# A two-layer encoder kernel: guest splits pinned to three points of each up-projection step, their stores on GpSimd's queue, and modulation dots moved beside the input projection

## The chip, the cores and the metric

The kernel runs on one core of a Trainium2 chip. The metric is the device time of one execution in microseconds. Three runs were timed and their median is used. A hardware profile of one further execution gives the busy times, waits and single instructions below. Engines are named as in the profile: PE is TensorE, PEld its weight loads, DVE is VectorE, ACT is ScalarE, POOL is GpSimd, SP is SyncE, which here only issues DMAs.

## The reference

The reference is an encoder of two layers over 1024 positions of 1024 channels. Each layer takes a modulation vector of six parts from a conditioning vector `c`, mixes along the sequence (attention in layer 0, a long-convolution mixer in layer 1), and then runs a gated feed-forward network whose gate passes a convolution of three taps.

```python
for i in range(DEPTH):
    mod = (silu(c) @ ada_w[i] + ada_b[i])[:, None, :]
    sh1, sc1, g1, sh2, sc2, g2 = jnp.split(mod, 6, axis=-1)
    h = rmsnorm(x, norm1_g[i]) * (1.0 + sc1) + sh1
    y = attention_mixer(h, ...) if i == 0 else hyena_mixer(h, ...)   # hyena starts with h @ w_in
    x = x + g1 * y
    h = rmsnorm(x, norm2_g[i]) * (1.0 + sc2) + sh2
    gate, val = jnp.split(h @ w_up, 2, axis=-1)
    x = x + g2 * ((silu(dwconv3(gate)) * val) @ w_down)
return rmsnorm(x, final_g)
```

## The kernel before

Everything is float32. A matrix product is made of three products of split operands: each operand is a high part (a cast on ScalarE, for weights `nc.scalar.copy`) and a low part (the difference, a `tensor_tensor` on VectorE, the helper `sub_lo`, L162), and the product of the two low parts is left out. The splits are therefore work for ScalarE and VectorE beside every product of TensorE.

The stages, in order of time: the input norm and the query, key and value projection (channels of weights in the order 2, 0, 1, each over eight tiles `j` of 128 positions); attention; the output projection `wo` over eight row tiles `dt_`; the feed-forward network of layer 0, which is `ffn(0, ...)`; the long-convolution mixer; `ffn(1, ...)`; the final norm.

*The up projection in `ffn`.* It goes over 22 tiles `f` of the hidden width. Two are made plainly. For the other 20 a step of seven products, `product(...)` at L946, gives gate and value with one product fewer (a scheme with sums and differences of the operands). A step loads its weights `u` through SP's queue, casts them in `fill` (L1033, `w_hi`) and subtracts (L162, `w_lo`), adds partial results (`pu`, `cv`), makes the convolution and the Silu of the gate (L287 to L289, L1002), and sends the product to memory (`sg`). The last product of a step and its gating, `late`, run inside the next step.

*Guests.* At three places of a step, `extra(...)` advances a generator once; the work in it is called a guest here. In layer 0 the generator is `l1_work`. It prepares weights of layer 1: 64 half tiles of `w_in` and `w_out` are loaded (`lo_load`, L1204, three buffers `wi_raw`), cast (L1218, `wi_hi`), subtracted (L1219) and their low parts stored to memory (L1220, `wld` and `wold`). 54 advances share the 64 splits, so some take two. In layer 1 the generator is `l1_mod5`, eight modulation dots.

*The order on each engine* comes from the framework's scheduler. It takes the instructions in the order in which the code issues them as their priority, follows a simulated timeline, and may put an instruction earlier on its engine than it stands in the code, where its inputs are there and its engine is free in that simulation. Each engine then runs its instructions in that fixed order. `tc.issue_after(ins)` adds a rule for the instructions issued within the block: those on the engine of `ins` come after `ins`. It does not bound them from above, and says nothing on other engines or on DMA queues.

*Modulation dots.* The 48 parts of layer 1's modulation (six vectors of eight columns) are each one `scalar_tensor_tensor` with a sum on VectorE (`mod_dot`, L197) of 512 KB of `ada_t` against the row silu(c). Where they run: 0 to 15 beside the output projection, two to a turn (`wide_dots`, in halves, L386); 16 to 39 beside the first down projection, after every second row tile; 40 to 47 as guests of the second up projection. In the third channel of the first projection GpSimd makes another modulation vector with `mod_step` (L185 to L190), which adds up in the tile `ssq`; the row of the dots is also held in `ssq`. The weights of a channel and the raw data of `mod_step` come through the same two buffers, `w_raw`.

*The down projection.* Row tiles `dt_` run over groups of hidden tiles; TensorE's sums `d_ps` are added to `xd` on VectorE (L1138). Beside the groups after the first the long filter of layer 1 is made (`filter_gen`: products `f_ps`, then L429 to L437 on VectorE, results to `ed`), one part after every second row tile. The weights of the last group (`wdt`) use the room of the filter's pool, so they are written once the filter is finished.

Of the kernel before, what the change touches and what calls it, by code (L numbers as in the profile page):

```python
# [53 lines left out]
L1_WO, L1_DN = 16, 40  # L54
# [61 lines left out]
def tile_kernel(ctx: ExitStack, tc: tile.TileContext, t: dict):  # L116
# [251 lines left out]
    def wide_dots(S, n):  # L368
        row, bufs = S[0:2], [S[2:4], S[4:6], S[6:8]]
        part = const.tile([P, n], F32, name="m_part")  # L370
# [7 lines left out]
        load(0)  # L378
        load(1)
        for j in range(n):  # L380
            if j + 2 < n:
                load(j + 2)
            i, k = divmod(j, KT)
            for hf, acc in enumerate((mod[:, 1, i, k:k + 1], part[:, j:j + 1])):
                w = bufs[j % 3][hf]
                V.scalar_tensor_tensor(w, w, 1.0, row[hf], op0=MUL, op1=MUL, accum_out=acc)  # L386
            if k == KT - 1:
                V.tensor_tensor(mod[:, 1, i], mod[:, 1, i], part[:, j - k:j + 1], op=ADD)
                mod_bias(1, i)
            yield  # L390
# [217 lines left out]
    with tc.tile_pool(name="qkv", bufs=1) as qp:  # L608
# [56 lines left out]
        todo = []  # L665

# [4 lines left out]
        for ch in (2, 0, 1):  # L671
            w = qkv_w if ch == 2 else [load_split(t["w_qkv"][ch, k2], wq, 4) for k2 in range(4)]
            if ch == 1:
                for k in range(KT):
                    mod_step(2, ssq, k)
            pqs = dict(enumerate(pq0)) if ch == 2 else {}
            for j in range(NT):
                if j not in pqs:
                    pqs[j] = mt("qkv_mm", {2: "AAAABBAA", 0: "AABBAAAA", 1: "AAAABBBB"}[ch][j])
                    tj = slice(j * P, (j + 1) * P)  # L680
                    for k in range(KT):
                        wh, wl = w[k // 2]
# [291 lines left out]
    def ffn(l, base, work, tail, more=None):  # L974
# [15 lines left out]
        fl = []  # L990
# [8 lines left out]
        def gated(f, cv):  # L999
            g = fp.tile([P, L], F32, name="gate", tag="gate")  # L1000
            dwconv(cv, [col(C_FW + (3 * l + i) * NF + f) for i in range(3)], col(C_FB + l * NF + f), g)
            nc.scalar.activation(g, g, AF.Silu)  # L1002
# [35 lines left out]
        for f in range(NPL[l], NF):  # L1038
# [10 lines left out]
            nc.scalar.copy(pu[:, 0], y1_[:, 0:512])  # L1049
# [38 lines left out]
        extra(48)  # L1088
# [34 lines left out]
        for j in range(len(ends) - 1):  # L1123
# [3 lines left out]
            for dt_ in range(KT):  # L1127
# [11 lines left out]
                if l == 0 and dt_ % 2:  # L1139
# [38 lines left out]
    def mod_load(i, pool=None):  # L1178
        raw = raw_tile() if pool is None else pool.tile([P, 1024], F32, name="m_raw", tag="m_raw", bufs=2)
        nc.sync.dma_start(raw, t["ada_t"][2 + i // KT, i % KT])  # L1180
        return raw

    def mod_dots(lo, hi, pool=None):
        w = mod_load(lo, pool)
        for i in range(lo, hi):
            w, wn = mod_load(i + 1, pool) if i < hi - 1 else None, w
            mod_dot(1, i // KT, i % KT, wn, ssq)
            if i % KT == KT - 1:
                mod_bias(1, i // KT)
            yield  # L1190

    def l1_mod5(pool, after):
        V.tensor_copy(ssq[0:1, 0:1], after[0:1, 0:1].bitcast(F32))
        silu_row(ssq)
        yield from mod_dots(L1_DN, 48)

    def l1_work(pool, after):
# [12 lines left out]
        for i in range(L1_STEPS):  # L1210
            while n < (i + 1) * len(los) // L1_STEPS:
# [8 lines left out]
                nc.sync.dma_start(dst[:, cs], raw)  # L1220
# [645 lines left out]
```

## Time and profile before

| | us |
|---|---|
| median of 3 runs | 2997.17 (2996.94 to 3002.17) |
| profiled execution, its own time | 3006.47 |
| span of the profile | 3004.7 |
| busy: TensorE | 2837.0 (94%) |
| busy: VectorE | 2333.3 (78%) |
| busy: ScalarE | 1231.0 (41%) |
| busy: GpSimd | 289.1 (10%) |

The span runs from the first to the last instruction of the profiled execution. A row of a timeline gives start and duration in microseconds, engine, line, operation, and in brackets how long the engine stood idle before it and what it waited for. A row of the waits gives total, number and longest. A row by stretch gives busy time and number of instructions of each engine in it, the granted clock of TensorE and the DMA engines' busy share. Starts are counted from the start of the span.

### The profile page before, as it was taken

Reading aid. Unit: us, or ns where it says so; the run is one execution under the profiler, and the core shown is the slowest. Engines: PE = TensorE matmul, PEld = TensorE weight load, DVE = VectorE, ACT = ScalarE, POOL = GpSimd, SP = SyncE. Lnnn points to the kernel's source line nnn. Section 1 sums busy time; section 2 is a strip of 40 time slices with the busy share of each in tenths; the row PEclk is TensorE's granted clock in tenths of the full one; section 3 lists DMA queues with packets and bytes.
Section 4 is the critical chain, followed back from the end, with each engine's and each line's share of the span. In section 5 each row is a group of like instructions: output and inputs, shape, how many; then the busy total and the mean of one; then the engine's idle time right before and its main releaser. Section 6 shows DMA issues by size and latency. Waiting matters only on the chain.

```text
span 3004.7 us, 36415 instructions
## 1 busy us (share of the span) xinstructions
PE 2837.0 (94%) x13152; PEld 2308.3 (77%) x13152; DVE 2333.3 (78%) x3212; ACT 1231.0 (41%) x2001; POOL 289.1 (10%) x292
## 2 busy tenths in 40 slices
PE   5989999999899999999889999999988999999998
PEld 4867877777777787888777877877867788887887
DVE  7788998867788777888677886788977977777544
ACT  3557888834444333343332233323333433333211
POOL 0064465300000000111000000000000000000000
PEclk9999999999999999999999999999999999999999
DMA  6252232162667323876446664556655422223321
GB/s 229 80 161 52 50 81 57 37 227 104 207 215 233 109 78 112 253 218 189 149 162 208 204 217 165 190 193 194 211 186 208 140 84 84 85 77 131 129 84 57
DMA packets 224777, 439.49 MB, mean 146 GB/s; under 512 B 22131, under 2 KB 117139, under 8 KB 220117
## 3 DMA queue, kind: packets, MB, share of 16 engines
q1 hardware_dynamic: 192788, 407.80, 40.1%
q0 software_dynamic: 31808, 29.37, 4.2%
q8 instruction: 104, 1.70, 0.2%
q14 instruction: 77, 0.62, 0.1%
HBM read 308.09 MB, written 128.99 MB: 145 GB/s over the span
## 4 chain that ended last, share of the span: by engine, by line
PE 55%; DVE 8%; DMA 8%; issue 2%; ACT 1%; SPq 0%; DVEq 0%; ACTq 0%; POOLq 0%
PE w_ps L946 20%; PE d_ps L181 16%; PE u_ps L1306 6%; PE ab_ps L1442 2%; DMA wld<-wi_raw 2%; PE f_ps L486 1%; PE f_ps L181 1%; PE f_ps L487 1%; PE z_ps L1420 1%; PE z_ps L1421 1%; DMA wi_raw<-in_w_in_dram 1%; DMA rd<-fw 1%; PE wout_y L181 1%; PE g_ps L283 1%; PE wout_y L1593 1%
## 5 line engine op out<-in xcount | busy, mean ns | idle before, releaser
L1033 ACT CAST w_hi<-u 128x1024 fp32r<-128x1024 f32 x120 | 125.5, 1047 | 203.8 <-PE w_ps L946 194.0
L162 DVE TENSOR_TENSOR pT_lo<-pt_ps,pT_hi 128x512 fp32r<-128x512 f32 x256 | 167.5, 680 | 46.8 <-ACT pT_hi L761 44.7
L946 PE MATMUL w_ps<-t_h,w_hi 128*128 128x512 f32 x480 | 193.2, 403 | 4.3 <-ACT w_hi L1033 4.0
L181 PE MATMUL d_ps<-s_hi,wd_lo 128*128 128x512 f32 x608 | 194.1, 390 | 0.0
L162 DVE TENSOR_TENSOR w_lo<-u,w_hi 128x1024 fp32r<-128x1024 f32 x120 | 146.6, 1222 | 60.2 <-ACT w_hi L1033 60.1
L181 PE MATMUL d_ps<-s_lo,wd_hi 128*128 128x512 f32 x608 | 193.3, 390 | 0.0
L181 PE MATMUL d_ps<-s_hi,wd_hi 128*128 128x512 f32 x608 | 193.0, 390 | 0.0
L946 PE MATMUL w_ps<-t_l,w_hi 128*128 128x512 f32 x480 | 192.1, 400 | 0.0
L946 PE MATMUL w_ps<-t_h,w_lo 128*128 128x512 f32 x480 | 191.2, 399 | 0.0
L1138 DVE SCALAR_TENSOR_TENSOR xd<-d_ps,mod,xd 128x1024 f32<-128x1024 f32 x104 | 132.6, 1279 | 71.8 <-PE d_ps L181 71.4
L761 ACT CAST pT_hi<-pt_ps 128x512 fp32r<-128x512 f32 x256 | 145.1, 589 | 70.7 <-PE pt_ps L756 63.4
L740 DVE TENSOR_REDUCE nmx<-s_ps 128x1 f32<-128x1024 f32 x128 | 155.4, 1215 | 11.1 <-PE s_ps L733 9.2
L756 PE MATMUL pt_ps<-ident,p_t 128*128 128x128 f32 x1024 | 154.6, 275 | 9.3 <-DVE pT_lo L162 9.0
L756 PEld LDWEIGHTS pt_ps<-ident,p_t 128*128 128x128 f32 x1024 | 126.7, 141 | 44.3 <-DVE pT_lo L162 8.2
L946 PE MATMUL w_ps<-fh_h,w_hi 128*128 128x512 f32 x320 | 127.2, 397 | 23.6 <-ACT w_hi L1033 22.2
L750 ACT ACTIVATE p_t<-s_ps,nmx 128x1024 f32<-128x1024 f32 x128 | 143.8, 1124 | 3.3 <-DVE nmx L740 2.1
L1306 PE MATMUL u_ps<-fh_h,w_lo 128*128 128x512 f32 x384 | 141.1, 423 | 2.3 <-DMA w_lo<-wld 2.3
L1306 PE MATMUL u_ps<-fh_l,w_hi 128*128 128x512 f32 x384 | 136.4, 419 | 2.3 <-DVE fh_l L239 2.3
L1306 PE MATMUL u_ps<-fh_h,w_hi 128*128 128x512 f32 x384 | 130.6, 414 | 3.4 <-ACT fh_h L238 3.4
L181 PEld LDWEIGHTS d_ps<-s_hi,wd_lo 128*128 128x128 f32 x608 | 113.6, 188 | 23.8 <-issue 0.9
L181 PEld LDWEIGHTS d_ps<-s_hi,wd_hi 128*128 128x128 f32 x608 | 113.8, 188 | 23.4 <-issue 0.4
L1442 PE MATMUL ab_ps<-prod,dfti 128*128 128x256 f32 x512 | 124.8, 387 | 7.1 <-DVE prod L1512 3.2
(402 smaller groups left out, 7453.4 us busy)
## 6 DMA issues: line engine op xcount, KB each, us to landing
u<-in_w_up_dram SPq DMA_DIRECT2D x80, 512.0 KB
w_raw<-in_w_down_dram SPq DMA_DIRECT2D x44, 512.0 KB
sg<-gate SPq DMA_DIRECT2D x40, 512.0 KB
w_raw<-sg SPq DMA_DIRECT2D x40, 512.0 KB
w_raw<-in_ada_w_dram SPq DMA_DIRECT2D x32, 512.0 KB
ed<-eo SPq DMA_DIRECT2D x64, 256.0 KB
eo<-ed SPq DMA_DIRECT2D x16, 1024.0 KB
kd<-k_sb SPq DMA_DIRECT2D x64, 256.0 KB
```

The costliest lines, as they stand in the source:

```text
L162: V.tensor_tensor(lo, src, hi.bitcast(F32), op=SUB)
L181: mm(out[:, cs], lhsT=a, rhs=b[:, cs], start=start and i == 0, stop=stop and i == 2)
L283: mm(pp[:, HS[hf]], lhsT=(wh, wh, wl)[i][:, ks], rhs=hd[hf][i % 2][k], start=k == 0 and i == 0, stop=k == n - 1 and i == 2)
L740: V.tensor_reduce(nmx, s_t[u, i], op=ALU.max, axis=AX.X, negate=True)
L750: nc.scalar.activation(p_t, s_ps, AF.Exp, bias=nmx, accum_out=sums[u][:, i:i + 1])
L756: nc.tensor.transpose(tp[:, i * P:(i + 1) * P], pts[u, i][:, sb * P:(sb + 1) * P], ident)
L761: nc.scalar.copy(ph, pt_t[u, sb][0])
L946: mm(out, lhsT=(w[0], w[0], w[1])[i][:, k * P:(k + 1) * P], rhs=b[i % 2][k], start=k == 0 and i == 0, stop=k == 3 and i == 2)
L1033: nc.scalar.copy(w[0], src)
L1138: ins = V.scalar_tensor_tensor(x[dt_], yp, gate[dt_], x[dt_], op0=MUL, op1=ADD)
L1306: mm(yp[:, HS[hf]], lhsT=(wh, wh, wl)[i][:, k * P:(k + 1) * P], rhs=hd[hf][i % 2][k], start=k == 0 and i == 0, stop=k == KT - 1 and i == 2)
L1442: mm(ap[:, i], lhsT=dfti[:, m, :], rhs=v, start=n == 0, stop=n == len(ops) - 1)
```

## The change

The guests of both up projections are put behind named instructions: the advance after the third and the one after the fifth product come, on ScalarE, after the copy of the first sum (`i_a`, L1049) and, on VectorE, after an addition of that place (`i_v`); the third advance comes after the gate's Silu and the last addition of `pu`. The guests' stores go through GpSimd's queue instead of SP's. In the second up projection a dot is followed by two empty advances, so one dot falls to a step.

The dots are divided anew: 0 to 11 beside the first projection (last four tiles of channel 2, all eight of channel 0), 12 to 31 beside the output projection, three to a turn, 32 to 39 in the first group of the down projection, 40 to 47 as before. The row silu(c) is loaded into `ssq` ahead of the first projection's loop, and all twelve dots are issued before `mod_step` starts there. `mod_load` and `mod_dots` move up in the file unchanged.

```diff
-L1_WO, L1_DN = 16, 40
+L1_Q, L1_WO, L1_DN = 12, 32, 40
...
-    def wide_dots(S, n):
+    def wide_dots(S, lo, hi):
...
         todo = []
+        silu_row(ssq)
+        dots = mod_dots(0, L1_Q)
...
             if ch == 1:
+                for _ in dots:
+                    pass
                 for k in range(KT):
                     mod_step(2, ssq, k)
...
+                if ch == 0 or ch == 2 and j > 3:
+                    next(dots, None)
...
-    dots = wide_dots(scratch[7:], L1_WO)
+    dots = wide_dots(scratch[7:], L1_Q, L1_WO)
...
-        for _ in range(L1_WO // KT):
-            next(dots)
+        for _ in range(3):
+            next(dots, None)
...
-        def extra(n):
+        def extra(n, a, v):
             for _ in range(n if extra_g else 0):
-                next(extra_g, None)
+                with tc.issue_after(a.ins), tc.issue_after(v.ins):
+                    next(extra_g, None)
...
-            nc.scalar.activation(g, g, AF.Silu)
+            g_ins[:] = [nc.scalar.activation(g, g, AF.Silu)]
...
-            nc.scalar.copy(pu[:, 0], y1_[:, 0:512])
+            i_a = nc.scalar.copy(pu[:, 0], y1_[:, 0:512])
...
-            V.tensor_tensor(pu[:, 1], pu[:, 0], y2[:, 512:1024], op=ADD)
-            extra(1)
+            i_v = V.tensor_tensor(pu[:, 1], pu[:, 0], y2[:, 512:1024], op=ADD)
+            extra(1, i_a, i_v)
             product(w5, T[1], y1_[:, 512:1024])
-            V.tensor_tensor(pu[:, 0], pu[:, 1], y1_[:, 512:1024], op=ADD)
+            i_v = V.tensor_tensor(pu[:, 0], pu[:, 1], y1_[:, 512:1024], op=ADD)
             product(w3, B22, y3[:, 0:512])
-            extra(1)
+            extra(1, i_a, i_v)
...
-            V.tensor_tensor(pu[:, 1], pu[:, 1], y3[:, 512:1024], op=ADD)
+            i_v = V.tensor_tensor(pu[:, 1], pu[:, 1], y3[:, 512:1024], op=ADD)
             if not end:
                 g = gated(f, cv[:, 0])
-            extra(EXN - 2)
+            extra(EXN - 2, g_ins[0], i_v)
...
-        extra(48)
+        for _ in extra_g or ():
+            pass
...
-                if l == 0 and dt_ % 2:
+                if l == 0 and j == 0:
                     with tc.issue_after(ins.ins):
                         next(dots, None)
...
-        yield from mod_dots(L1_DN, 48)
+        for _ in mod_dots(L1_DN, 48):
+            yield
+            yield
+            yield
...
-                nc.sync.dma_start(dst[:, cs], raw)
+                nc.gpsimd.dma_start(dst[:, cs], raw)
```

More of the change, by code (lines that the diff above doesn't have):

```diff
@@ L366, in filter_mlp, with mod_load, mod_dots @@
         yield
-    def wide_dots(S, n):
+    def mod_load(i, pool=None):
+        raw = raw_tile() if pool is None else pool.tile([P, 1024], F32, name="m_raw", tag="m_raw", bufs=2)
+        nc.sync.dma_start(raw, t["ada_t"][2 + i // KT, i % KT])
+        return raw
+    def mod_dots(lo, hi, pool=None):
+        w = mod_load(lo, pool)
+        for i in range(lo, hi):
+            w, wn = mod_load(i + 1, pool) if i < hi - 1 else None, w
+            mod_dot(1, i // KT, i % KT, wn, ssq)
+            if i % KT == KT - 1:
+                mod_bias(1, i // KT)
+            yield
+    def wide_dots(S, lo, hi):
         row, bufs = S[0:2], [S[2:4], S[4:6], S[6:8]]
-        part = const.tile([P, n], F32, name="m_part")
+        part = const.tile([P, hi - lo], F32, name="m_part")
         for hf in range(2):
@@ L377, in load @@
                 nc.sync.dma_start(bufs[j % 3][hf], t["ada_t"][2 + j // KT, j % KT][:, HS[hf]])
[L378 to L381, printed above, removed]
+        load(lo)
+        load(lo + 1)
+        k0 = lo % KT
+        for j in range(lo, hi):
+            if j + 2 < hi:
                 load(j + 2)
             i, k = divmod(j, KT)
-            for hf, acc in enumerate((mod[:, 1, i, k:k + 1], part[:, j:j + 1])):
+            for hf, acc in enumerate((mod[:, 1, i, k:k + 1], part[:, j - lo:j - lo + 1])):
                 w = bufs[j % 3][hf]
@@ L387, in wide_dots @@
             if k == KT - 1:
-                V.tensor_tensor(mod[:, 1, i], mod[:, 1, i], part[:, j - k:j + 1], op=ADD)
+                V.tensor_tensor(mod[:, 1, i, k0:], mod[:, 1, i, k0:], part[:, j - lo - k + k0:j - lo + 1], op=ADD)
                 mod_bias(1, i)
+                k0 = 0
             yield
@@ L989, in ffn @@
         gate = [mod[:, l, 5, d:d + 1] for d in range(KT)]
-        fl = []
+        fl, g_ins = [], []
         def split(g, pool):
@@ L1176, in ffn @@
         s0.release()
[L1178 to L1190, printed above, removed]
     def l1_mod5(pool, after):
@@ L1194, in l1_mod5 @@
         silu_row(ssq)
-        yield from mod_dots(L1_DN, 48)
+        for _ in mod_dots(L1_DN, 48):
+            yield
+            yield
+            yield
     def l1_work(pool, after):
```

## The prediction

> **What bounds the kernel now.** I read the page first, then the busy time by stage, then the step times of the two up projections, then who waited for whom inside the slow stretch, and last the end of the first down projection.
>
> ```profile
> span 3004.7 us, 36415 instructions
> PE 2837.0 (94%) x13152; PEld 2308.3 (77%) x13152; DVE 2333.3 (78%) x3212; ACT 1231.0 (41%) x2001; POOL 289.1 (10%) x292
> ```
>
> TensorE is the bound, so only microseconds in which it stands idle, or runs at a lower clock after standing idle, can be won. The next view gives, by stretch, busy time of each engine, granted clock and DMA share.
>
> ```profile
> core 0: us, PE busy (x) PEld busy (x) DVE busy (x) ACT busy (x) POOL busy (x), PEclk, DMA share, GB/s
> 85.00:135.00 50.00, 50.00 (x258) 42.10 (x257) 34.45 (x77) 29.24 (x103) 0.00 (x0) 1.00 0.13 43
> 780.00:1003.00 223.00, 202.50 (x840) 160.86 (x840) 181.12 (x231) 97.99 (x132) 0.00 (x0) 0.96 0.63 210
> 1022.00:1177.00 155.00, 155.00 (x675) 126.19 (x674) 116.95 (x135) 52.39 (x58) 0.00 (x0) 1.00 0.21 72
> 1199.00:1222.00 23.00, 22.83 (x99) 18.53 (x100) 20.95 (x24) 8.25 (x13) 5.04 (x10) 1.00 0.92 296
> 1222.00:1460.00 238.00, 238.00 (x1208) 198.84 (x1207) 192.75 (x251) 85.81 (x136) 29.75 (x56) 1.00 0.66 201
> 1460.00:1480.00 20.00, 11.19 (x54) 7.57 (x54) 11.16 (x19) 7.30 (x12) 0.00 (x0) 0.78 0.27 80
> ```
>
> 780 to 1003 and 1022 to 1177 are the same loop, the first up projection, with and without guest splits (L1218, L1219). With them TensorE misses 20.5 us and the clock falls to 0.96; without them it never stops. Each step makes one copy on L1049, so these copies time the steps (start, us; the first four of the first up projection, the last four of the second):
>
> ```profile
> 779.58 0.58 ACT L1049 COPY pu<-w_ps 128x512 f32<-128x512 f32 x1
> ...
> 1002.73 0.59 ACT L1049 COPY pu<-w_ps 128x512 f32<-128x512 f32 x1
> ...
> 1022.27 0.59 ACT L1049 COPY pu<-w_ps 128x512 f32<-128x512 f32 x1
> ...
> 1176.80 0.59 ACT L1049 COPY pu<-w_ps 128x512 f32<-128x512 f32 x1
> ...
> 2355.84 0.59 ACT L1049 COPY pu<-w_ps 128x512 f32<-128x512 f32 x1 [1.55 <-PE w_ps L946]
> 2381.82 0.59 ACT L1049 COPY pu<-w_ps 128x512 f32<-128x512 f32 x1 [1.14 <-DVE cv L1085]
> 2403.72 0.59 ACT L1049 COPY pu<-w_ps 128x512 f32<-128x512 f32 x1
> ...
> 2733.53 0.59 ACT L1049 COPY pu<-w_ps 128x512 f32<-128x512 f32 x1
> ```
>
> Ten steps with guests take 223.15 us, 22.3 each; eight without take 154.53, 19.32 each. In the second projection two steps take 25.98 and 21.90 and the next seventeen 19.40 each. Why a guest costs TensorE time stands in ScalarE's order:
>
> ```profile
> 806.27 0.62 ACT L1218 CAST wi_hi<-wi_raw 128x512 fp32r<-128x512 f32 x1 [3.50 <-DMA wi_raw<-in_w_in_dram]
> 806.80 1.05 ACT L1002 ACTIVATE gate<-gate 128x1024 f32<-128x1024 f32 x1
> 807.76 1.03 ACT L1033 CAST w_hi<-u 128x1024 fp32r<-128x1024 f32 x1
> ...
> 808.84 0.79 PE L946 MATMUL w_ps<-fh_h,w_hi 128*128 128x512 f32 x1 [5.39 <-ACT w_hi L1033]
> ACT wi_hi L1218 <- DMA wi_raw<-in_w_in_dram: 58.0, 19, 8.3
> ```
>
> ```profile
> L1218 ACT CAST wi_hi<-wi_raw x64: 601/620/626, 769.7 to 984.7; 128x512 fp32r<-128x512 f32 x64
> L1219 DVE TENSOR_TENSOR wi_raw<-wi_raw,wi_hi x64: 677/686/694, 771.0 to 985.4; 128x512 fp32r<-128x512 f32 x64
> ```
>
> The guest's cast waited 3.50 us for its load; the cast of the step's own weights stood behind it, and TensorE stood 5.39 us. The guests run back to back as fast as their three buffers recycle (that is why all 64 are over by 986 us, in eleven steps of eighteen), so nearly every cast meets a load in flight: 19 waits, 58.0 us.
>
> **The change part by part.**
>
> *Guests pinned to three points, their stores on GpSimd's queue.* What a buffer's round takes (two transfers of the chain, then the loads that GpSimd issues elsewhere):
>
> ```profile
> 798.10 5.41 DMA wld<-wi_raw
> 803.53 2.67 DMA wi_raw<-in_w_in_dram
> L1590 POOL DMA_DIRECT2D wo_l<-wold x8: 528/531/558, 2062.8 to 2225.1; - x8
> DMA to landing us min/median/max: 3.2/5.4/8.9
> ```
>
> 64 splits over 18 steps are 3.56 a step: 2.44 us of VectorE (0.686 each) and 2.21 us of ScalarE (0.62). A step without guests holds 116.95/155 x 19.32 = 14.6 us of VectorE and 6.5 of ScalarE, so 17.0 and 8.7 of 19.32: both fit. Behind a pinned cast on ScalarE stand the step's weight casts and its Silu, behind a pinned subtraction the weights' low parts; both are only harmed if the pinned instruction itself has to wait. It waits if its buffer is not back. A round is store 5.41 (on the GpSimd queue by the nearest row, loads of the same 256 KB, 5.4, at most 8.9), load 2.67, split 1.31: 9.4, at most 12.9 us. Three buffers at one split per 19.32/3.56 = 5.43 us allow 16.3. So the loads should have landed. The 64 stores leave SP's queue, where the weight loads of the steps stand behind each, and put 64 x 0.53 = 34 us on GpSimd, idle throughout (0.00 in both stretches). Ten intervals fall from 223.15 to 193.2 us, a gain of 29.95. I give back 2.5 us for the start of the stage, where earlier splits still fill VectorE, and 2 for small delays over 18 steps: **-25.5** (ends -30 and, with a residue of 0.7 us a step, -17.5).
>
> The Trainium skill, "SBUF — State Buffer", in its summary of rules, speaks against the new queue: a DMA issued from GpSimd is starved of descriptors while VectorE runs certain modes, so the hardware queue is to be preferred under VectorE work. Its section "Who interferes with whom" holds, as an inference, that instructions with two tensors in do not starve them, and this stage's large VectorE work is of that form. The trace has 56 GpSimd operations beside 192.75 us of VectorE in 1222 to 1460, and the dots there (next rows) are no longer than elsewhere. By the page's warning each store would lengthen by what VectorE instruction it meets, about 1.3 us; 12.9 becomes 14.2 of 16.3, and the sum stays.
>
> *Modulation dots.* One costs 1.215 + 0.081 = 1.296 us of VectorE:
>
> ```profile
> L197 DVE SCALAR_TENSOR_TENSOR m_raw<-m_raw,ssq x24: 1210/1215/1218, 1209.7 to 1420.5; 128x1024 f32<-128x1024 f32 x24
> L197 DVE DVE_READ_ACCUMULATOR m_raw<-m_raw,ssq x24: 78/81/84, 1210.9 to 1421.7; 128x1 f32 x24
> ...
> L197 DVE SCALAR_TENSOR_TENSOR w_raw<-w_raw,ssq x8: 1215/1218/1226, 2353.1 to 2372.2; 128x1024 f32<-128x1024 f32 x8
> ```
>
> Second up projection: eight dots stood in its first three steps (2353 to 2372) and now go one to a step, beside 14.6 us of other VectorE work. The first two intervals, 47.88, should fall to 2 x 19.40 plus the same 2.5: **-6.6** (ends -9.1 and -3).
>
> First down projection: 24 dots become 8, all in the first group. Twenty leave the stretch in which the filter is made, 25.9 us of VectorE. TensorE is full there, so this is worth nothing until the end:
>
> ```profile
> 1228.90 1.28 DVE L429 TENSOR_TENSOR eo<-f_ps,dec 128x512 f32<-128x512 f32 x2
> ...
> 1415.30 0.68 DVE L429 TENSOR_TENSOR eo<-f_ps,dec 128x512 f32<-128x512 f32 x1
> 1429.18 0.69 DVE L429 TENSOR_TENSOR eo<-f_ps,dec 128x512 f32<-128x512 f32 x1
> ...
> 1468.20 0.69 DVE L429 TENSOR_TENSOR eo<-f_ps,dec 128x512 f32<-128x512 f32 x1 [0.73 <-DMA ed<-eo]
> ...
> 1477.01 1.99 ACT L169 CAST wd_hi<-w_raw 128x1024 fp32r<-128x1024 f32 x2 [2.27 <-DMA skd<-srow]
> ...
> 1461.99 1.18 PE d_ps L181 x5
> ...
> 1478.13 6.56 PE d_ps L181 x21
> ```
>
> TensorE ran out of down products at 1463.17 and had the last group's only at 1478.13, because their weights (cast at 1477.01) take the room of the filter, whose last products were made at 1468.20. Of the 15 us TensorE was idle 8.8 (20 - 11.19), and the clock fell to 0.78. Three quarters of the filter beside the dots took 186.4 us, 62 each; the last, without dots, 39. If VectorE's load is what slows it, the filter ends up to 25.9 - 5.2 = 20.7 us sooner and the stall goes (late next: nothing, the products run on). Ends -12 (idle plus clock) and 0 (the pace is TensorE's order); nearer to the first, since 39 against 62 is the row that differs by the dots: **-8**.
>
> First group of down: four more dots, 5.2 us, in 23 us that had 2.05 us of VectorE left. 3.1 do not fit and push the next group's splits; TensorE has four sums open in PSUM to go on with. Ends 0 and +5.2: **+2**.
>
> Input projection: 12 dots, 15.6 us of VectorE, twelve loads of 512 KB and one of the row on SP's queue (DMA share 0.13), one Silu on ScalarE (29.24 of 50 busy). VectorE's gaps from 85 to 135 are 50 - 34.45 = 15.55 us: just enough. The loads take the two buffers through which the next weights come. And the third channel's GpSimd work now waits until the last dot has read its row. That work disturbs VectorE already:
>
> ```profile
> 158.58 5.82 DVE L627 TENSOR_TENSOR qk_b<-qk_n,Tq 128x256 f32<-128x256 f32 x2
> ...
> 159.15 4.96 POOL L190 TENSOR_TENSOR ssq<-ssq,w_raw 128x1024 f32<-128x1024 f32 x2
> ```
>
> Two products took 5.82 us, as long as GpSimd's two additions ran. The dots cannot meet those additions, which write the row that dots read; starting later only moves the disturbance. Ends +15.6 (no gap takes a dot) and -3 (a disturbance falls behind the stage); nearer to the hidden end, as the gaps are there: **+2**. The Trainium skill, same page, "Who interferes with whom", states the mechanism: a VectorE instruction with two SBUF inputs and a GpSimd one that reads SBUF lock each other out for their whole length; the row above agrees. By it each of the seven additions moved costs VectorE the same as before, so the sum is the same.
>
> Output projection: 20 dots instead of 16, three to a turn, on a full TensorE; four dots are 5.2 us. Ends 0 and +5.2: **+1**.
>
> **Sum:** -25.5 - 6.6 - 8 + 2 + 2 + 1 = -35.1. The profiled execution (span 3004.7) took 3006.47 us, 0.3% over the median of 2997.17; against the latter the forecast is **2962 us**.
>
> **The rivals.** (B) The filter's pace is TensorE's order, not VectorE: the 8 us stay, 2970. For it: TensorE was full until 1460. Against: 39 us beside 62.
> (C) The dots beside the input projection are not absorbed: 13.6 us more, 2976. For it: room of 15.55 for 15.6. Against: TensorE lost nothing in that stretch.
> (D) The pins do not spread the guests: a pin says only "not before", so guests may bunch at later points, and half of the first term goes: 2975. For it: nothing here bounds them from above. Against: ScalarE's room, 10 us a step.
> (F) The other side: the pinned cast meets its load late in every step, because a buffer's round on the GpSimd queue exceeds 16.3 us, and each of 18 steps costs the 22.3 us that the ten cost. Then the first term is 8 x 3.0 = +24 in place of -25.5, and the total is +14: 3012. It decides against the change from 2.2 us a step on (18 x 2.2 = 39.6, the gain of 29.95 and the other terms' 9.6). Against it: at most 8.9 us to landing.
> (E) B, C and D together bring it to 2996, no change.
>
> **How the numbers follow.** About 0.2%, 6 us, is what a measurement of this kernel tells from no change. Forecast 0.52, B 0.15, C 0.10, D 0.08 are all faster: 0.85. E 0.05 is the same; F 0.10 is slower. The low end takes the best of each term, -30 - 9.1 - 12 = -51: 2946. The high end takes C or D at 2976 with some of the other bounds (first term -17.5, second -3, filter 0, costs +8): -12, 2985. Left out are E, F and a little of D.
>
> **What would show it.** Steps of 19.3 to 19.6 us from 780 to 1177 with casts of the guests spread up to about 1150, and their waits for loads gone from the list of waits; if these waits remain, the first term is wrong. The first two steps at 2355 near 20; the stretch that was 1460 to 1480 without idle TensorE, or B holds. The projections ahead of attention show C if TensorE's idle time there has grown by more than 5 us. A late weight load or cast that TensorE waits for in each step would mean F.

## The result, and the profile after

The changed kernel takes 2964.4 us (median of four runs, 2959.88 to 2967.2) against 2999.67 us of the kernel before, run beside it (four runs, 2996.94 to 3003.09): a ratio of 0.988, 95% interval 0.9862 to 0.9899, a gain of 35.3 us. The forecast was 2962 (2946 to 2985). A second group of runs gave 0.9876 (0.9858 to 0.9895).

The head of the page of the changed kernel; this execution took 2959.88 us:

```profile
span 2958.1 us, 36525 instructions
PE 2821.6 (95%) x13152; PEld 2299.2 (78%) x13152; DVE 2331.2 (79%) x3221; ACT 1232.8 (42%) x2004; POOL 324.9 (11%) x356
```

TensorE's instructions are the same 13152; its busy time fell by 15.4 us, which fits the fewer stretches at a lowered clock (the mean granted clock rose from 0.980 to 0.985), and the rest of the 46.6 us between the two spans is idle time that went. Busy time by stretch after the change, columns as in the prediction, the stretches shifted with their stages (1434 to 1454 is the new place of the old stretch 1460 to 1480):

```profile
core 0: us, PE busy (x) PEld busy (x) DVE busy (x) ACT busy (x) POOL busy (x), PEclk, DMA share, GB/s
85.00:135.00 50.00, 50.00 (x254) 42.09 (x254) 43.65 (x104) 29.76 (x105) 0.00 (x0) 1.00 0.37 116
780.00:1003.00 223.00, 223.00 (x972) 182.19 (x971) 192.47 (x239) 97.60 (x122) 21.21 (x39) 1.00 0.52 174
1022.00:1160.00 138.00, 138.00 (x601) 112.70 (x600) 115.30 (x140) 57.64 (x71) 11.86 (x22) 1.00 0.43 147
1173.00:1196.00 23.00, 22.57 (x97) 18.32 (x98) 20.69 (x24) 9.17 (x13) 5.24 (x10) 1.00 0.92 296
1196.00:1434.00 238.00, 238.00 (x1218) 197.76 (x1217) 181.51 (x229) 89.83 (x145) 29.74 (x56) 1.00 0.57 173
1434.00:1454.00 20.00, 20.00 (x88) 15.62 (x87) 13.56 (x18) 7.20 (x10) 0.00 (x0) 1.00 0.46 132
```

From 780 to 1003 TensorE was busy 202.50 of 223 us before, and is busy all of it now, at full clock. The stall before the last down group (11.19 of 20) is gone. The copies of the first sum, which time the steps (L1072 is the old L1049), in the first up projection and at the start of the second:

```profile
780.96 0.59 ACT L1072 COPY pu<-w_ps 128x512 f32<-128x512 f32 x1 [2.70 <-PE w_ps L968]
...
1151.04 0.59 ACT L1072 COPY pu<-w_ps 128x512 f32<-128x512 f32 x1
...
2316.51 0.59 ACT L1072 COPY pu<-w_ps 128x512 f32<-128x512 f32 x1 [0.99 <-PE w_ps L968]
2337.87 0.59 ACT L1072 COPY pu<-w_ps 128x512 f32<-128x512 f32 x1 [1.46 <-DVE cv L1108]
2358.73 0.59 ACT L1072 COPY pu<-w_ps 128x512 f32<-128x512 f32 x1
```

Nineteen intervals take 370.08 us, 19.48 each; before they took 397.22. The guests' casts and stores, and ScalarE's waits for their loads (58.0 and 22.4 us before):

```profile
L1231 ACT CAST wi_hi<-wi_raw x64: 600/620/626, 781.4 to 1132.9; 128x512 fp32r<-128x512 f32 x64
L1233 POOL DMA_DIRECT2D wld<-wi_raw x48: 542/542/594, 793.9 to 1045.2; - x48
DMA to landing us min/median/max: 2.3/2.6/5.9
```

```profile
ACT wi_hi L1231 <- DMA wi_raw<-in_w_in_dram: 1.6, 1, 1.6
```

The casts are spread to 1132.9. All but the first two intervals take 19.0 to 19.4 us; those two take 19.79 and 22.35. For the books by stage, the first and the last products of the two up projections and of the first down projection, of the kernel before and then of the changed one (each row ends with the start of the first and of the last product of its kind):

```profile
L946 PE MATMUL w_ps<-fh_h,w_hi x320: 387/389/792, 771.3 to 1191.9; 128*128 128x512 f32 x160
L946 PE MATMUL w_ps<-fh_h,w_lo x320: 388/389/628, 773.1 to 1192.3; 128*128 128x512 f32 x160
L181 PE MATMUL d_ps<-u,wd_lo x32: 388/388/398, 1481.5 to 1503.7; 128*128 128x512 f32 x32
L946 PE MATMUL w_ps<-gh_h,w_hi x320: 387/389/628, 2352.9 to 2748.6; 128*128 128x512 f32 x160
L946 PE MATMUL w_ps<-gh_h,w_lo x320: 387/389/398, 2353.3 to 2749.1; 128*128 128x512 f32 x160
```

```profile
L968 PE MATMUL w_ps<-fh_h,w_hi x320: 388/389/497, 775.9 to 1166.1; 128*128 128x512 f32 x160
L968 PE MATMUL w_ps<-fh_h,w_lo x320: 388/389/497, 778.4 to 1166.6; 128*128 128x512 f32 x160
L181 PE MATMUL d_ps<-u,wd_lo x32: 388/392/397, 1444.1 to 1466.7; 128*128 128x512 f32 x32
L968 PE MATMUL w_ps<-gh_h,w_hi x320: 388/389/398, 2313.6 to 2701.8; 128*128 128x512 f32 x160
L968 PE MATMUL w_ps<-gh_h,w_lo x320: 388/389/397, 2314.0 to 2702.3; 128*128 128x512 f32 x160
```

| stage, from these rows | before, us | after, us | difference |
|---|---|---|---|
| start to the first product of the first up projection | 771.3 | 775.9 | +4.6 |
| first up projection | 421.0 | 390.7 | -30.3 |
| first down projection (to its last product) | 311.4 | 300.1 | -11.3 |
| long-convolution mixer, to the second up projection | 849.2 | 846.9 | -2.3 |
| second up projection | 396.2 | 388.7 | -7.5 |

The mixer is not touched by the change. Over the fourteen profiles of this study it took 844.0 to 853.4 us, with the same code, so its -2.3 says nothing; differences of a stage as large as that are read only where several profiles agree. The first row, too, hides something: before the change the first product waited 3.5 us for its weight cast, `w_hi`, behind guests. So the row holds a little of the guests' gain beside the cost of the moved dots.

### The profile page after: what moved, and what is told of

It reads as the page before. It is cut to its first block, busy times and chain, and to the rows that moved or that the text cites. A ratio compares the mean times of both kernels' runs of the same rounds, so it can differ in the third digit from the quotient of the medians.

```text
span 2958.1 us, 36525 instructions
## 1 busy us (share of the span) xinstructions
PE 2821.6 (95%) x13152; PEld 2299.2 (78%) x13152; DVE 2331.2 (79%) x3221; ACT 1232.8 (42%) x2004; POOL 324.9 (11%) x356
## 4 chain that ended last, share of the span: by engine, by line
PE 65%; DVE 8%; DMA 3%; issue 1%; ACT 1%; SPq 0%; DVEq 0%; ACTq 0%; POOLq 0%
PE w_ps L968 26%; PE d_ps L181 16%; PE u_ps L1319 5%; PE wo_y L181 3%; PE ab_ps L1455 2%; PE g_ps L283 2%; PE f_ps L181 2%; PE v_ps L283 2%; PE f_ps L502 1%; PE f_ps L503 1%; DVE prod L1525 1%; DMA rd<-fw 1%; PE wout_y L181 1%; PE z_ps L1433 1%; PE wout_y L1606 1%
## 5 line engine op out<-in xcount | busy, mean ns | idle before, releaser
L181 PEld LDWEIGHTS d_ps<-s_lo,wd_hi 128*128 128x128 f32 x608 | 113.5, 188 | 24.3 <-issue 1.3
```

What stands on the lines that cost most here:

```text
L181: mm(out[:, cs], lhsT=a, rhs=b[:, cs], start=start and i == 0, stop=stop and i == 2)
```

## The experiments

Each edit is one to the changed kernel unless it says otherwise. "Stage" times are taken from the same rows as in the table.

**The guests: pins or queue?** Two runs each undo one part.

```diff
-                nc.gpsimd.dma_start(dst[:, cs], raw)
+                nc.sync.dma_start(dst[:, cs], raw)
```

> The changed kernel with one part undone: the guests' low parts go to memory through SP's queue again, the pins stay. Theory of the prediction (the gain of the first up projection is the spreading; the queue matters little): the products of the first up projection take 390 us from first to last as in the changed kernel (390.7), within 3 us, the guests' casts reach past 1100 us, and the total stays at 2964 within 6 us. Rival (the stores on SP's queue, each waiting there for its subtraction with the weight loads behind it, were the cause): the stage takes 400 to 421 us, with waits for the step's weight loads or the guests' loads in the list, and the total is 2974 to 2994.

Measured: first up projection 390.7 us, casts up to 1133.8, total 2963.15 us, ratio to before 0.9849 (0.9836 to 0.9862). With the pins, the queue makes no difference to this stage, and the total is the expected one.

```diff
-                with tc.issue_after(a.ins), tc.issue_after(v.ins):
-                    next(extra_g, None)
+                next(extra_g, None)
```

> The changed kernel with the other part undone: no pins on the guests (nor on the dots of the second up projection), their stores stay on GpSimd's queue. Theory of the prediction (without the pins the guests run back to back as fast as the buffers recycle, and each cast that meets a load in flight holds the step's own weight casts behind it): all guests are over by about 990 us, ScalarE's waits for their loads are back at 40 us or more in sum, the stage takes 410 to 421 us and the total is 2984 to 2994. Rival (with the stores off SP's queue the loads land in time, so dense guests cost nothing): the stage takes 391 to 397 us and the total stays below 2972.

Measured: 2977.35 us, ratio 0.9893 (0.988 to 0.9907). The first up projection takes 395.4 us, inside the rival's 391 to 397, although all guests are over by 983 and ScalarE waits 70.4 us for their loads, as the theory had it; the total lies between the two forecasts (below 2972, and 2984 to 2994), and 5.8 us of it are lost in the second up projection, which has no pins here either. Neither won: dense guests with long waits cost TensorE only this much (stretch 780 to 1003 of the kernel without pins):

```profile
780.00:1003.00 223.00, 220.76 (x951) 177.53 (x950) 201.52 (x258) 107.79 (x143) 34.66 (x64) 1.00 0.65 225
```

So each part alone wins most of the stage. The control undoes both:

> The changed kernel with both the pins and the queue undone, only the dots as changed. Theory formed from the two runs that undid one of them (without pins six guests stand in each step's stretch of ScalarE's order, so a step lasts at least six guests; a guest costs about 3.4 us with both DMAs on SP's queue, where a load that waits for a store's landing holds back the next store, and 3.2 us with the stores elsewhere, just under the step): steps of 20.5 to 23 us while guests last, the stage 412 to 424 us, total 2985 to 2995. Rival (the old dots were part of the loss): the stage stays below 400 us and the total below 2975.

Measured: 2987.32 us, ratio 0.9947 (0.9931 to 0.9963), stage 413.4 us, both as expected; steps of 20.9 to 22.9 us but one of 27.4. TensorE's loss is back:

```profile
780.00:1003.00 223.00, 207.80 (x867) 165.90 (x866) 187.44 (x242) 100.03 (x135) 0.00 (x0) 0.97 0.66 222
```

Of the 30.3 us, then, pins or queue account for 22.7 (413.4 - 390.7); the other 7.6 came with the rest of the change (the places of the dots alter the order in which the stage starts) and were not traced further. That split is not a fixed price: with the pins, the old places of the dots cost only 2.1 us in this stage (392.8 in a run below).

The theory of a pace (a step lasts as long as the guests that stand in it) was tried by changing the time of a guest, without and with pins:

```diff
-LPB = 3
+LPB = 2
```

> As the kernel without pins and without the new queue, and with two buffers for the guests' weights in place of three. Theory (without pins a step lasts as long as the guests that stand in it, and a guest lasts a buffer's round divided by the number of buffers): the guest's time goes from 3.4 to between 4.4 and 5.2 us, steps with six guests take 26 to 31 us, the stage 450 to 500 us and the total 3025 to 3075. Rival (TensorE is held by something else, the buffers are not the bound): the stage stays within 10 us of the version with three buffers.

Measured: 2982.16 us, ratio 0.9936 (0.9917 to 0.9955), stage 407.5 us: shorter than with three buffers by 5.9 us, where the theory said 40 to 90 longer and the rival no more than 10 apart. The guest's time did rise, from 3.40 to 4.22 us (64 casts from 776.8 to 1042.8), but the scheduler then put five guests in a step, not six.

> The changed kernel (pins and GpSimd's queue) with two buffers for the guests in place of three. Theory: a round of store 2.6, load 2.7 and split 1.3 us, with waits some 8 us, allows a split each 4 us, and the pins ask for one in 5.4: nothing changes, stage within 2 us of 390.7, total 2964 within 6 us. Rival F of the prediction (a pinned cast that meets its load late stops the step) at this size: steps of 21 us or more, stage 425 us, total 3000.

Measured: 2964.39 us, ratio 0.9871 (0.9853 to 0.9889), stage 390.6 us. The number came out as expected but its reason did not: the pinned casts do meet their loads late, and TensorE loses nothing by it. Waits and the stretch, of the pinned kernel with two buffers:

```profile
ACT wi_hi L1231 <- DMA wi_raw<-in_w_in_dram: 45.7, 19, 3.7
ACT wi_hi L1231 <- DMA wi_raw<-in_w_out_dram: 18.0, 6, 4.7
```

```profile
780.00:1003.00 223.00, 223.00 (x971) 182.31 (x970) 191.17 (x236) 96.12 (x122) 21.14 (x39) 1.00 0.50 175
```

What TensorE itself waited for sorts the versions. These are its waits for the casts of its own weights over the whole execution (total, number, longest), of the kernel before, of "neither", of "neither" with two buffers, and of the kernel without pins:

```profile
PE w_ps L946 <- ACT w_hi L1033: 26.2, 10, 5.4
PE w_ps L968 <- ACT w_hi L1055: 16.6, 8, 4.0
PE w_ps L968 <- ACT w_hi L1055: 15.3, 11, 4.0
PE w_ps L968 <- ACT w_hi L1055: 6.8, 6, 4.0
```

In each, one wait of 4.0 us belongs to the start of the second up projection; the table has what is left for the first (before, 3.5 us of it lie just ahead of its first product). The pinned kernels have one wait of 0.7 us there.

| version | guests in most steps | us a guest (casts, first to last, by 63) | median step with guests | ScalarE's waits for guests' loads | TensorE's waits for its weight casts | stage |
|---|---|---|---|---|---|---|
| before | 6 | 3.41 | 22.3 | 80.4 | 22.2 | 421.0 |
| neither | 6 | 3.40 | 22.4 | 81.1 | 12.6 | 413.4 |
| neither, two buffers | 5 | 4.22 | 20.4 | 115.0 | 11.3 | 407.5 |
| no pins, GpSimd's queue | 6 | 3.25 | 20.1 | 70.4 | 2.8 | 395.4 |
| pins, SP's queue | 3 or 4 | not bound | 19.3 | none listed | 0.7 | 390.7 |
| pins, two buffers | 3 or 4 | not bound | 19.3 | 63.7 | 0.7 | 390.6 |

The guests' waits for loads do not order the stages: 63.7 us of them cost nothing, 70.4 cost 4.7, 81.1 cost 22.7 and 115.0 cost 16.8. The number of guests in a step does not either: six cost 30.3, 22.7 or 4.7 us, five cost 16.8. TensorE's waits for its own weight casts do, and they make up somewhat over half of each loss; the granted clock from 780 to 1003 goes the same way (0.96, 0.97, 0.98 and 1.00 in the four versions without pins, 1.00 with them). So the loss comes in where the prediction saw it, at a weight cast that ScalarE makes late. It is not a late load of these weights: from 768 to 1195 the profile lists no cast that waits for one, and VectorE waits for them 3.1 us in "neither", 1.8 before, and not at all in the other two versions without pins. Why TensorE's waits fall from 12.6 to 2.8 us when the guests' stores go to GpSimd's queue, with as many guests in a step, stays open. The time of a guest can't decide it, since it is taken from the same steps: with six guests in each step, six times that time is the length of a step, whichever of the two sets the pace.

**The dots of the second up projection.**

```diff
-        for _ in mod_dots(L1_DN, 48):
-            yield
-            yield
-            yield
+        yield from mod_dots(L1_DN, 48)
```

> The changed kernel with the dots of the second up projection three to a step again, as before, but pinned. In the runs without pins these dots ran at the very start of the stage although the code gave one to a step. Theory (the pins carry the whole of that term): 14.6 + 3 x 1.3 = 18.5 us of VectorE fit into a step of 19.3, TensorE loses nothing, the first two intervals are 40 to 43 us and the total is 2964 within 6 us. Rival (one dot to a step is what won it, as the prediction had it): the first two intervals are 46 to 48 us and the stage is 4 to 7 us longer.

Measured: 2964.56 us, ratio 0.9866 (0.9846 to 0.9886); the first two intervals are 42.1 us (22.73 and 19.35; 42.2 in the changed kernel) and the stage 388.7 us, the same to 0.1 us as with one dot to a step. The pins carry this term. The three runs without pins took 394.4 to 394.5 us in this stage though their code does give one dot to a step. The eight dots of the kernel without pins, of the changed one, and of the pinned one with three to a step:

```profile
L197 DVE SCALAR_TENSOR_TENSOR w_raw<-w_raw,ssq x8: 1211/1214/1227, 2320.7 to 2339.9; 128x1024 f32<-128x1024 f32 x8
```

```profile
L197 DVE SCALAR_TENSOR_TENSOR w_raw<-w_raw,ssq x8: 1216/1219/1221, 2334.8 to 2459.6; 128x1024 f32<-128x1024 f32 x8
```

```profile
L197 DVE SCALAR_TENSOR_TENSOR w_raw<-w_raw,ssq x8: 1215/1218/1221, 2342.5 to 2376.6; 128x1024 f32<-128x1024 f32 x8
```

Empty advances in the code had moved nothing: without a pin the scheduler took the dots ahead, all eight into the first 20 us of the stage, as before.

**The other dots.** First, all of them where they were:

```diff
-L1_Q, L1_WO, L1_DN = 12, 32, 40
+L1_Q, L1_WO, L1_DN = 0, 16, 40
...
-        silu_row(ssq)
-        dots = mod_dots(0, L1_Q)
+        dots = iter(())
...
-        for _ in range(3):
+        for _ in range(2):
...
-                if l == 0 and j == 0:
+                if l == 0 and dt_ % 2:
```

> The changed kernel with the dots where they were before: none beside the first projection, 0 to 15 beside the output projection, 16 to 39 after every second row tile of the down projection. Theory of the prediction (VectorE's load of dots slows the filter, which holds the last group's weights): the idle stretch of TensorE at the end of the down projection is back, that stage is 8 to 12 us longer, the projections ahead of attention are 4 to 5 us shorter of which attention takes most away, and the total is 2970 to 2976. Rival (the filter's pace is the order of the products on TensorE): no stall comes back, and the total falls by the cost of the moved dots, to 2958 to 2962.

Measured: 2966.37 us, ratio 0.9859 (0.9842 to 0.9876), 3.2 us over the version with stores on SP in the same group. That is below the forecast band of 2970 to 2976: the down projection is 11.5 us longer (311.6), as expected, but the work ahead of the first up projection is 6.6 us shorter, more than the 4 to 5 expected. (In its one profile the two up projections are also 2.1 and 1.7 us longer; the stages of that profile sum to more than the 3.2 us of the medians, whose four runs spread from 2960.12 to 2972.0.) The stall is back:

```profile
1437.00:1456.00 19.00, 10.84 (x36) 6.62 (x35) 8.64 (x14) 5.54 (x9) 0.00 (x0) 0.73 0.34 97
```

Is it VectorE's time, or the dots' loads? Two edits to the kernel before. The first leaves out most of each sum, for the dots of the down projection alone:

```diff
-            mod_dot(1, i // KT, i % KT, wn, ssq)
+            cs = slice(0, 1024 if pool is None else 8)
+            mod_dot(1, i // KT, i % KT, wn[:, cs], ssq[:, cs])
```

> The kernel before, with the 24 dots of its first down projection cut to 8 of their 1024 columns: the rest of these sums is left out, their loads of 512 KB, their places in the order and their waits stay. Theory of the prediction (VectorE's time for the dots slows the filter, and the last group's weights wait for the filter): the filter ends 15 to 25 us sooner in its stage, TensorE's stall before the last group is gone, and the down projection is 8 to 12 us shorter. Rival (the loads do it: SP stands 46.6 us for buffers of dots, with the filter's stores and the weights' loads queued behind): the stage stays within 3 us of before.

Measured: 2995.55 us, ratio to before 0.9959 (0.9943 to 0.9975); the down projection takes 299.8 us, 11.6 less.

The second leaves out all loads of these dots but the first:

```diff
-        raw = raw_tile() if pool is None else pool.tile([P, 1024], F32, name="m_raw", tag="m_raw", bufs=2)
+        raw = raw_tile() if pool is None else pool.tile([P, 1024], F32, name="m_raw", tag="m_raw", bufs=1 if pool else 2)
...
-            w, wn = mod_load(i + 1, pool) if i < hi - 1 else None, w
-            mod_dot(1, i // KT, i % KT, wn, ssq)
+            if pool is None:
+                w, wn = mod_load(i + 1, pool) if i < hi - 1 else None, w
+                mod_dot(1, i // KT, i % KT, wn, ssq)
+            else:
+                wn = pool.tile([P, 1024], F32, name="m_out", tag="m_out", bufs=1)
+                V.scalar_tensor_tensor(wn, w, 1.0, ssq, op0=MUL, op1=MUL, accum_out=mod[:, 1, i // KT, i % KT:i % KT + 1])
```

> The kernel before, with all 24 dots of its first down projection on one piece of weights, loaded once: 23 loads of 512 KB and their waits on SP are left out, VectorE's work is as before. Theory of the prediction (VectorE's time): the stall stays and the stage is within 3 us of before. Rival (the loads): the stall is gone, the stage 8 to 12 us shorter.

Measured: 3003.06 us, ratio 0.9996 (0.998 to 1.0011); the stage takes 307.8 us, 3.6 less (the theory had allowed 3). The filter's 64 products with the decay, first and last start, in the changed kernel, with short dots, and without the loads (before: 1228.9 to 1468.2):

```profile
L445 DVE TENSOR_TENSOR eo<-f_ps,dec x64: 679/684/693, 1203.2 to 1427.6; 128x512 f32<-128x512 f32 x64
```

```profile
L429 DVE TENSOR_TENSOR eo<-f_ps,dec x64: 669/684/692, 1230.4 to 1452.0; 128x512 f32<-128x512 f32 x64
```

```profile
L429 DVE TENSOR_TENSOR eo<-f_ps,dec x64: 672/684/692, 1221.2 to 1461.0; 128x512 f32<-128x512 f32 x64
```

239.3 us before; 224.4, 221.6 and 239.8. Without the loads the filter is no faster, and TensorE still waits at the end for the filter's last small transfers (timeline of the kernel without the loads):

```profile
1463.96 1.02 PE L442 MATMUL f_ps<-macc,ones 128*1 128x256 f32 x4 [2.52 <-DVE macc L437]
...
1468.82 1.65 PE L181 MATMUL d_ps<-u,wd_hi 128*128 128x512 f32 x3 [3.84 <-DMA scol<-sd]
```

VectorE's time is the cause; the loads account for no more than the 3.6 us.

**Where the dots have room.** Two variants move dots from the first projection to the output projection.

```diff
-L1_Q, L1_WO, L1_DN = 12, 32, 40
+L1_Q, L1_WO, L1_DN = 8, 32, 40
...
-                if ch == 0 or ch == 2 and j > 3:
+                if ch == 0:
```

> A variant: beside the first projection only eight dots, one to each tile of channel 0 and none beside channel 2; the other four go to the output projection, which then has 24, three to each of its eight turns. Theory (TensorE's new gaps from 40 to 100 us come from the dots beside channel 2 and the loads they take from the two weight buffers): the last product of that projection ends 2 to 4.5 us earlier, attention hands on 0 to 2 us of it, the output projection is 0 to 2 us longer: 2960 to 2966 in all. Rival (the gaps come from the dots of channel 0 or from the row's load ahead of the loop): the projection ends as in the changed kernel and the total is 2964 to 2970.

Measured: 2955.63 us, ratio 0.9824 (0.981 to 0.9837), the fastest version here and below its own forecast of 2960 to 2966: 7.5 us under the one with stores on SP in the same group, whose interval it just touches. The last product of the first projection ends at 198.6 us (203.7 in the changed kernel), the first up projection begins at 770.0. From 40 to 100 us, the changed kernel and then this one (before: 54.54 us):

```profile
40.00:100.00 60.00, 49.55 (x207) 38.73 (x206) 52.97 (x117) 23.81 (x56) 0.00 (x0) 0.94 0.37 121
```

```profile
40.00:100.00 60.00, 54.16 (x236) 43.32 (x235) 51.09 (x116) 25.65 (x64) 0.00 (x0) 0.94 0.27 94
```

The first projection's dots run at these times in the changed kernel and in this one:

```profile
L197 DVE SCALAR_TENSOR_TENSOR w_raw<-w_raw,ssq x12: 1217/1226/1226, 51.1 to 117.7; 128x1024 f32<-128x1024 f32 x12
```

```profile
L197 DVE SCALAR_TENSOR_TENSOR w_raw<-w_raw,ssq x8: 1214/1226/1227, 96.4 to 115.9; 128x1024 f32<-128x1024 f32 x8
```

The dots beside channel 2 cost TensorE 4.6 us there. Those beside channel 0 cost nothing that shows: the last product ends at 198.6 us, and with the old dots at 194.4 to 199.2.

```diff
-L1_Q, L1_WO, L1_DN = 12, 32, 40
+L1_Q, L1_WO, L1_DN = 0, 32, 40
...
-        silu_row(ssq)
-        dots = mod_dots(0, L1_Q)
+        dots = iter(())
...
-        for _ in range(3):
+        for _ in range(4):
```

> A variant: no dots beside the first projection, 32 beside the output projection, four to a turn. The variant with eight and 24 gained 8 us on the changed kernel. Theory (the output projection has room, its eight turns are 100 us with 85 to 90 us of VectorE work in them): up to the first up projection it ends where the kernel before does or 1 us sooner, and the total is 2954 to 2960. Rival (VectorE is full there, 39 of 40 us from 640 to 680, so twelve more dots cost their 15.6 us or half of it): the output projection is 6 to 15 us longer and the total is 2964 to 2972.

Measured: 2965.03 us, ratio 0.9868 (0.9849 to 0.9887), in the rival's band, above the theory's, and within 0.5 us of the pinned version of that group with the changed kernel's dots. Both projections end 5.3 us earlier than in the changed kernel, so the output projection is no longer with 32 dots beside it and the rival is wrong on the place; but the dots run on behind it, on VectorE, and the next norm waits for them:

```profile
L401 DVE SCALAR_TENSOR_TENSOR fh_l<-fh_l,fh_h x32: 670/674/691, 634.1 to 724.9; 128x512 f32<-128x512 f32 x32
```

```profile
PE g_ps L283 <- DVE fh_l L239: 8.6, 2, 7.8
```

TensorE's first products after it wait 8.6 us for VectorE (1.7 in the changed kernel), which gives back what the first projection had won.

**The spread of the runs.**

> The changed kernel once more, on the chip of this group. It should stand at 0.985 to 0.990 of the kernel before. Its profile shows how far the stages that the change does not touch (attention above all) move from one profiled run to the next: 2 to 5 us by the runs so far, so differences of that size there carry no verdict.

Measured: 2966.4 us. Its rows in the table by stage agree with the first profile of the changed kernel within 0.1 us, but for the mixer, which took 853.1 us against 846.9. The gain over before was 35.3 and 36.4 us in the two groups; the versions whose touched stages are the same within some 2 us gave 45.1 (stores on SP), 42.3 (dense dots) and 38.4 (two buffers) in their groups, since the kernel before moved from 2999.67 to 3008.2 between groups (the three groups of experiments ran on three chips). The stage sums below are of that size.

## Why the prediction came out right, step by step

The number was right, 2962 for 2964.4, with two terms too small and one cost too small.

- *First up projection, -25.5 forecast, -30.3 measured*, the low end of its range. The intervals between the copies, which it priced, won 27.1 us; most of what was given back is in the second of them (22.35 us, five guests). Another 3.2 us came ahead of the first copy (8.3 us after the first product before, 5.1 now), which the sum had left out. The forecast steps are there after the first two, and the casts reach 1132.9 where about 1150 was forecast. The price was read as "ten steps with guests, 22.3 us each"; in fact nine intervals hold guests, the first with ten of them takes 29.63 us, and the tenth, without any, 16.52. The price was right to 5 us, but the cause given for it was only half of one. That late weight casts on ScalarE stop TensorE is borne out. That they are late by the guests' waits for loads in flight is not: pinned casts with 63.7 us of such waits cost nothing, and dense guests with 70.4 us cost 4.7. And the two parts of the edit are substitutes, which the prediction did not see: it put the gain on the pins and gave the queue only the round's time.
- *Second up projection, -6.6 forecast, -7.5 measured.* In the two intervals that were priced 5.7 us came (47.88 to 42.22). The step "now go one to a step" is right in what happened and wrong in what did it: with pins three to a step take the same 388.7 us, and without pins one to a step takes 394.5.
- *End of the filter, -8, and first down group, +2; together -6 forecast, -11.3 measured.* The filter ends 14.9 us sooner in its stretch (the bound was 20.7), and the whole stall went, as 39 us beside 62 had suggested; the value belonged near its end of -12. The first group's cost is mis-sized: TensorE is busy 22.57 of 23 us there, 22.83 before, so 0.3 us and not 2.
- *The projections, +2 and +1 forecast, +7.2 measured.* In eight profiles with the changed kernel's dots the first up projection begins at 774.0 to 779.6 us (mean 776.65), in four with the old dots at 765.4 to 771.9 (mean 769.5). The first projection's last product moved by the same 6.9 (204.2 against 197.3, means of the same profiles), and the output projection's by 6.2, so the four dots more beside the output projection cost nothing that shows. (By the last product of the two plain tiles the difference is 9.3 us; those tiles take 2.7 us longer, which was not traced, and the shorter wait for the first step's weights gives 2.1 back.) The step that failed is the place: the prediction counted VectorE's gaps from 85 to 135 us, and there TensorE indeed loses nothing (50.00 of 50), but the dots and their loads begin earlier, at 51.1 us, in a stretch where TensorE already waited for the split input. Whether it is the dots' VectorE time there or the weight buffers they occupy was not tried apart.

The four differences are -4.8, -0.9, -5.3 and +4.2; the measured sum is -41.9, the five timed gains 35.3 to 45.1. So the number came out on its place partly because errors of opposite sign met, and partly by luck: the 35.3 of the first group is the smallest of the five.

The rivals: B (the filter's pace is TensorE's order) is refuted by the run with short dots. C in the full size of 13.6 us did not come, half of it did, and its sign is at its mark: 5.0 us more without work on TensorE from 40 to 100 (54.54 us busy before, 49.55 after). D (pins do not spread) is wrong, the casts run to 1132.9. F did not happen, and its pricing was wrong too: the pinned kernel with two buffers has a late load in 25 of 64 casts, up to 4.7 us, and most of its steps stay at 19.3; that ScalarE is busy for less than half of the time (96.12 of 223 us) fits this.

The Trainium skill's warning that was weighed ("SBUF — State Buffer", summary of rules: DMAs issued from GpSimd starve beside certain VectorE work) did not show here: the stores landed in 2.6 us (median; 5.9 at most) while VectorE was 86% busy (192.47 of 223). That VectorE work is mostly of instructions with two tensors in, which its section "Who interferes with whom" holds harmless, as an inference; the trace agrees with that.

## What to carry to other kernels

Where side work shares an engine with the work that feeds the bound engine, judge it by what the bound engine waits for: here these waits (22.2, 12.6, 11.3, 2.8 and 0.7 us) put the versions in the order of their stage times, while the side work's own waits and the number of its pieces in a step did not. Spreading side work by the place it has in the code does nothing if the scheduler may take it ahead; a rule "not before" on a named instruction did it alone, for two different kinds of work. And a piece of work moved under a full TensorE has to be followed to the stretch where it really runs: here it cost nothing where VectorE's gaps had been counted, and 5 us some thirty microseconds earlier.

## What the runs showed of the hardware that was not expected

A DMA issued on GpSimd cost 542 ns of GpSimd. The guests' stores of 256 KB landed after 2.3/2.6/5.9 us (min, median, max) from there, at a DMA share of 0.52, and without the pins, at a share of 0.65, after 2.3/3.2/6.4. On SP's queue one store on the chain before took 5.41 us (share 0.63); the one listing of landing times there, of the kernel without the dots' loads, has 2.0/3.7/5.4 (share 0.64). So the short times go at least in part with the less crowded stretch, and a faster queue is not shown. Stages with the same code moved by up to 9.4 us from profile to profile (the mixer, 844.0 to 853.4 us), while the pinned first up projection, where TensorE is full, took 390.7 us in four profiles (the changed kernel twice, stores on SP's queue, dense dots) and 389.5 to 392.8 in all eight with pins.
